# A hybrid attention block on one core: helper work moved in the prologue and the first slots, pairs turned in one transfer, and another order of the last products

## The chip, the cores and the metric

The kernel runs on one core of a Trainium2 chip. Five engines work side by side and wait for one another by semaphores: TensorE (PE; its weight loads are listed apart as PEld), VectorE (DVE), ScalarE (ACT), GpSimd (POOL) and SyncE (SP), which here issues the DMAs, plain ones and transposes. Each engine takes its instructions in the order in which they were written for it. The metric is the time of one execution on the device, in microseconds (us).

## The reference

x is 2048 rows of 1024 float32. It is normalised (RMS norm with a gain) and projected at once to the queries, keys and values of two attention mixers, to gates, and to merge gates:

```python
PROJ_SIZES = (A_WIDTH, A_KV_HEADS * HEAD_DIM, A_KV_HEADS * HEAD_DIM,
              len(B_GROUPS) * B_WIDTH, len(B_GROUPS) * B_WIDTH, len(B_GROUPS) * B_WIDTH,
              A_WIDTH, B_WIDTH, N_BRANCHES * D_MODEL)
```

Mixer A is a banded attention of 8 query heads over 2 key heads (window 128 to each side) with a sink logit; mixer B has three groups of 8 heads with dilations 1, 4 and 16, whose results are combined by their softmax denominators. Queries and keys get an RMS norm per head; a relative-position bias is added to the logits. Each mixer's output is gated, projected to 1024 columns, weighted by the merge gates, added up, and a last projection of it is added to x.

## The kernel before

Every matrix product is done in fp16 in three parts: each operand is split into a high and a low half (names ending in h and l, or XH and XL for the normalised x), and high x high, high x low and low x high are added up in PSUM. The program has these stages.

*Prologue* (0 to about 80 us). x is loaded in 16 tiles, normalised (xt, L462), turned by TensorE (L482), and split into XH by ScalarE (L485) and XL by VectorE (L489). Two pieces of the gate projection (L352) run between. The functions `x_again` (GpSimd copies the first columns of XH and XL behind the last ones, since a shifted unit reads past the end), `head_gain` (the rows by which the heads' norms are weighted, some ten small VectorE operations a call) and `small_scales` are helpers. A small planner, the class `Order`, is given each step with its engine, an assumed duration, what it depends on and a rank, and writes the steps out in the order that results.

*Attention* in units of 8 slots. An A unit holds four query heads and one key head, a B unit two heads of one dilation; the first three units are A, B, A. In each slot TensorE projects one pair of 128-row subsets (L697). The queries and keys of it are normalised (rw, spl, with GpSimd's steps L764 and L779) and turned by DMA transposes into the tiles kq by `Pair.turn` (L787). Then come the items of earlier pairs: logits s<-kq (L847), row maxima (L862), exponentials, high and low half p (L879), the DMA transpose of p to pt (L885), the values pv<-vt,pt (L896), and later the output: z and zd, yo, ya, and a turn on TensorE pt<-idf,ya (L960) into the bank also used for small column sums (pt<-ym,ones at L189), which VectorE reads in the gate L967.

Helpers that belong to no slot are put into a heap by `at(t, ...)` with a time counted in slots, and each is written out when the written-out work has come so far. The tables at the head of the file (W_STEP, Y_MAX, L_LAST and others) hold these times. So the order in which an engine, or SyncE's queue, gets its work follows from those numbers. The transposes of pair k are written at slot k + 2.24. The loads of the raw weights of the next unit (wraw, L178, four pieces of 384 KB, written two by two) stand at 0.1 and 0.6 slots into a unit. Squares of them, for the scale of their high half, follow at 1.9.

*Middle and last stage.* Seven-product matrix multiplication (Strassen's) with the two branch projections and the output projection. Classes `Branch` (L1921) and `Out` (L1993) hold seven products each; `run(g)` writes them as 0, 1, 2, 3, 4 and leaves 5 and 6 in a list `pending`, from which `late()` takes one between products of the next group, and `flush()` the rest. Products 0, 1 and 2 start a fresh bank of PSUM, 3, 5 and 6 add to the bank of product 0, and 4 to that of 2. After each product VectorE or ScalarE reads the bank (`after`): in `Out` it is added to a tile xr of x (L2000), which is then stored (L2003).

Of the kernel before, what the change touches and what calls it, by code (L numbers as in the profile page):

```python
# [21 lines left out]
F32 = mybir.dt.float32  # L22
F16 = mybir.dt.float16
# [11 lines left out]
HD = 64  # L35
# [10 lines left out]
def unit_order():  # L46
    us = [("A", 0, 0)]
    for p in range(4):
        us.append(("B", p, 1))
        if p == 0:  # L50
# [20 lines left out]
W_STEP = (0.1, 0.6, 1.9, 0.445, 4.186, 0.117, 0.301)  # L71
W_MAX = (3.542, 3.596)
G_PREP = (5.907,)
N_PREP = (5.948, 6.756, 7.277)
Y_MAX = (0.02, 0.445, 0.485)
# [7 lines left out]
W_RAW, L_LAST = 14.0, 0.3  # L83
# [16 lines left out]
            gh=1.06, gl=1.26, mm=.217, th=.6, gt=.63, us=.83, uh=.75, ul=.82, ag=1.0, tl=1.3)  # L100
XT_BUFS = 14
KQ_BUFS = 6
# [6 lines left out]
def block_kernel(tc, x, w_units, w_gate, w_mrg, w_out, w_bra, w_brk, gain, qkg, sink, bias_a, bias_b, b_merge, out):  # L109
# [301 lines left out]
    qg = sp0.tile([128, 4, HD], F32, name="qg")  # L411
# [148 lines left out]
    for t in range(NT):  # L560
# [15 lines left out]
        if t < 2:  # L576
            for k in range(2):
                od.add(("ag", t, k), "G", us_["ag"], [("lo", t, 1)], 0, x_again, t, (XH, XL)[k])
# [37 lines left out]
    od.add("h0", "V", 1.6, [("st", groups[7])], 170, head_gain, 0, first=46.0)  # L616
    od.add("h1", "V", 1.6, ["h0"], 170, head_gain, 1)
    od.add("ss", "V", .2, ["h1"], 171, small_scales)
# [61 lines left out]
    class Pair:  # L680
# [100 lines left out]
        def turn(self):  # L781
            for i, s in enumerate(self.subsets):
                if self.un.shift and s[1] == 0:
                    kq = wk.tile([128, 6, 128], F16, name="kq0", bufs=3)
                else:
                    kq = wk.tile([128, 6, 128], F16, name="kq", bufs=KQ_BUFS)
                nc.sync.dma_start_transpose(out=kq[:], in_=self.sp[:, i].rearrange("p a b c -> p (a b c)"))  # L787
                self.un.kq[s] = kq
# [415 lines left out]

    ws, fill = {}, {}
    w_forms(NU + SEQ[0][0], 8 * NU)
    for u in range(NU + 1):
        t = 8 * u
        steps = [(t + W_STEP[i], w_load, u + 1, (2 * i, 2 * i + 1)) for i in range(2)]
        for i in range(4):  # L1210
            steps.append((t + W_STEP[2] + W_STEP[3] * i, w_square, u + 1, i))
# [662 lines left out]
    def run(g):  # L1874
        emit(g, 0)
        if g.n == 1:
            late()
            return
        emit(g, 1)
        late()  # L1880
        emit(g, 2)
        emit(g, 3)
        late()
        emit(g, 4)
        pending.extend(((g, 5), (g, 6)))
# [89 lines left out]
    class Out(Seven):  # L1975
# [11 lines left out]
        def matmuls(self, i, ps, fresh):  # L1987
            m = mf[self.s, i]
            out = []
            for p in range(4):  # L1990
# [14 lines left out]

        def after(self, i):
            b = self.b
            for h, n, k, store in (((0, 0, 0, False),), ((1, 1, 2, False),), ((0, 0, 1, True),), ((0, 1, 0, False),),
# [7 lines left out]
    def AB(s):  # L2016
# [7 lines left out]
        run(Branch(s, 1))  # L2024
# [98 lines left out]
```

## Time and profile before

| | us |
|---|---|
| Median of 3 runs | 1914.71 (1913.5 to 1917.62) |
| The profiled execution | 1916.55 |
| its span, first to last instruction | 1914.3 |
| TensorE busy in it | 1873.9 |
| VectorE, ScalarE, GpSimd busy | 1500.7, 1250.4, 579.0 |

The mean granted clock of TensorE was 0.999. A row of a timeline holds the start, the duration, the engine, the line, the operation, the tiles (out<-in), the shape, the count, and in brackets the idle time ahead of it with what ended it. Rows of SPq are what SyncE itself needs to issue a DMA; when the data lands is listed apart. A line of the list of waits has the idle time in all, how often, and the longest.

### The profile page before, as it was taken

To read this page: it belongs to the slowest core of one execution; us is meant where nothing else is said; L and a number is where in the kernel's file an instruction comes from. 1 tells how busy PE (TensorE), PEld (TensorE's weight loads), DVE (VectorE), ACT (ScalarE), POOL (GpSimd) and SP (SyncE) were. 2 spreads that over 40 slices of the span, in tenths; PEclk is the share of its full clock that TensorE was granted. 3 is DMA by queue.
4 is the path that set the end of the run, shared out by engine and by line. 5 is a ranking of instruction groups with operands and counts; after the bars stand their busy time and mean duration, and the time that the engine had idled before them with its cause. 6 is when DMAs were issued, how large, how long until landed. Compare 5 with 4: busy or idle time off the path is not lost.

```text
span 1914.3 us, 51103 instructions
## 1 busy us (share of the span) xinstructions
PE 1873.9 (98%) x19242; PEld 1438.9 (75%) x19242; DVE 1500.7 (78%) x3835; ACT 1250.4 (65%) x3015; POOL 579.0 (30%) x1363
## 2 busy tenths in 40 slices
PE   6999999999999999999999999999999999999998
PEld 4567887889999899998999899544444446776774
DVE  7679878986887879878788888748679644987885
ACT  8577768887676777777776766565666865433431
POOL 1034343443454435534455444300000001322121
PEclk9999999999999999999999999999999999999999
DMA  6259998988889679888897777786666648854541
GB/s 256 83 98 197 164 185 134 192 161 178 149 161 181 134 158 200 151 170 169 143 179 144 147 154 132 165 309 172 211 198 188 190 156 273 290 164 122 148 148 65
DMA packets 639351, 326.21 MB, mean 170 GB/s; under 512 B 459264, under 2 KB 589952, under 8 KB 636672
## 3 DMA queue, kind: packets, MB, share of 16 engines
q1 hardware_dynamic: 638960, 322.70, 73.3%
q8 instruction: 150, 2.46, 0.6%
q14 instruction: 97, 0.79, 0.2%
q10 hardware_dynamic: 144, 0.26, 0.0%
HBM read 139.08 MB, written 73.66 MB: 111 GB/s over the span
## 4 chain that ended last, share of the span: by engine, by line
PE 90%; DMA 5%; DVE 2%; ACT 1%; issue 1%; POOL 0%; SPq 0%; DVEq 0%; POOLq 0%
PE pj L697 43%; PE fps L1602 17%; PE fps L1921 8%; PE fps L1993 8%; PE s L847 5%; PE pv L896 4%; DMA pt<-p 2%; PE pj L352 2%; PE pj L304 1%; PE fps L304 1%; DMA kq<-spl 1%; PE pt L960 1%; DMA bigl<-sd 1%; DVE pr L862 0%; PE s L482 0%
## 5 line engine op out<-in xcount | busy, mean ns | idle before, releaser
L697 PE MATMUL pj<-wl,XH 128*128 128x128 f16 (+2 forms) x2816 | 715.8, 268 | 0.0
L697 PE MATMUL pj<-wh,XL 128*128 128x128 f16 (+2 forms) x2816 | 712.2, 269 | 0.0
L697 PE MATMUL pj<-wh,XH 128*128 128x128 f16 (+2 forms) x2816 | 709.4, 268 | 0.0
L697 PEld LDWEIGHTS <-XH 128*128 128x128 f16 x5632 | 575.3, 112 | 54.5
L697 PEld LDWEIGHTS <-XL 128*128 128x128 f16 x2816 | 315.9, 112 | 24.0
L862 DVE CUSTOM_DVE_ANT_0 pr<-s,b,ubuf 128x256 f32<-128x256 f32 (+3 forms) x512 | 218.9, 465 | 44.1 <-PE s L847 41.7
L879 DVE SCALAR_TENSOR_TENSOR p<-pr,p 128x512 f16<-128x512 f32 (+2 forms) x256 | 195.7, 765 | 51.6 <-ACT p L875 50.4
L764 POOL TENSOR_TENSOR rw<-rw,g 128x128 f32<-128x128 f32 (+1 forms) x224 | 149.1, 686 | 202.5 <-DVE rw L757 183.2
L1931 POOL TENSOR_TENSOR g<-g,t 128x512 f32<-128x512 f32 x32 | 48.8, 1526 | 523.7 <-DVE t L1854 523.7
L1602 PEld LDWEIGHTS <-wh 128*128 128x128 f16 x1064 | 104.1, 99 | 123.5 <-issue 0.4
L715 ACT ACTIVATE rw<-pj 128x256 f32<-128x256 f32 (+1 forms) x224 | 87.5, 390 | 134.5 <-PE pj L697 134.0
L779 POOL COPY spl<-spl 128x256 f16<-128x256 f16 (+1 forms) x224 | 96.4, 460 | 246.5 <-DVE spl L774 246.5
L875 ACT ACTIVATE p<-pr 128x512 f16<-128x512 f32 (+2 forms) x256 | 157.7, 616 | 14.4 <-DMA pt<-p 10.1
L1921 PE MATMUL fps<-y,bigh 128*128 128x128 f16 x1792 | 153.5, 219 | 0.8 <-DVE r L1854 0.8
L847 PE MATMUL s<-kq 128*128 128x128 f16 (+1 forms) x1856 | 148.2, 218 | 4.8 <-DMA kq<-spl 3.9
L1921 PE MATMUL fps<-y,bigl 128*128 128x128 f16 x896 | 151.7, 219 | 0.0
L1993 PE MATMUL fps<-WO,mf 128*128 128x512 f16 x672 | 150.3, 379 | 0.8 <-DVE xr L2000 0.8
L847 PEld LDWEIGHTS <-kq 128*128 128x128 f16 x2016 | 131.0, 98 | 21.1 <-issue 5.7
L1921 PEld LDWEIGHTS <-bigh 128*128 128x128 f16 x1792 | 139.0, 98 | 8.2 <-issue 0.9
L896 PE MATMUL pv<-vt,pt 128*128 128x65 f16 (+1 forms) x2784 | 132.1, 193 | 8.7 <-DMA pt<-p 7.7
L896 PEld LDWEIGHTS <-pt 128*128 128x128 f16 x3024 | 119.6, 98 | 24.6 <-DMA pt<-p 12.5
L770 ACT ACTIVATE spl<-rw 128x512 f16<-128x512 f32 (+1 forms) x112 | 72.1, 643 | 79.7 <-POOL vt L726 71.4
(252 smaller groups left out, 3815.0 us busy)
## 6 DMA issues: line engine op xcount, KB each, us to landing
wraw<-in_w_units_dram SPq DMA_DIRECT2D x56, 384.0 KB, 4.8
g<-mgd SPq DMA_DIRECT2D x64, 256.0 KB, 5.4
wraw<-in_w_mrg_dram SPq DMA_DIRECT2D x45, 256.0 KB, 4.2
mgd<-t SPq DMA_DIRECT2D x43, 256.0 KB, 2.9
zd<-z SPq DMA_DIRECT2D x128, 66.0 KB, 2.0
zz<-zd SPq DMA_DIRECT2D x64, 132.0 KB, 3.5
xt<-in_x_dram SPq DMA_DIRECT2D x16, 512.0 KB, 7.8
ytd<-yo SPq DMA_DIRECT2D x32, 256.0 KB, 3.5
```

Source lines behind the costliest of these rows:

```text
L697: out.append(lambda lhs=lhs, rhs=rhs, ch=ch, a=a, b=b, k=k: T.matmul(ps[:, a:b], lhsT=lhs[:, ch, :], rhs=rhs[:, ch, a:b], start=(k == 0), ...
L715: A.activation(self.rw[:, n * i:n * i + n], self.ps[i][:, :n], AF.Copy)
L764: G.tensor_tensor(q[:, i, :un.nq, :], q[:, i, :un.nq, :], g, OP.mult)
L779: G.tensor_copy(sp[:, i, nh:, :, :], sp[:, i, nq:nh, ::-1, :])
L847: T.matmul(self.sv[j][:, o:o + k1 - k0], lhsT=q[:, h, :], rhs=kt[:, un.nq + kh + v * un.nk, k0:k1], start=(v == 0), stop=(v == 1))
L862: V.tensor_tensor_reduce(out=self.pv[:, j, self.p0:self.p0 + W], in0=self.sv[j], in1=un.bias[:, self.h0 + j, self.b0:self.b0 + W], scale=I ...
L875: A.activation(self.sp[:, :128 * n], self.pr, AF.Copy, scale=PSC)
L879: V.scalar_tensor_tensor(self.sp[:, 128 * n:], self.pr, PSC, self.sp[:, :128 * n], OP.mult, OP.subtract)
L896: T.matmul(self.po[:, j, :w], lhsT=p[:, n * j + s, :], rhs=un.v[key][:, vh, c0:c0 + w], start=(k == 0 and s == 0), stop=(k == 2 and s == n ...
L1602: T.matmul(b[k][:], lhsT=w[:, i, ch, :], rhs=xform(PROD[i][0], lo, ch, q), start=(i < 3 and n == 0), stop=(n == 11), skip_group_check=True)
L1921: out.append(lambda p=p, c=c, wl=wl, yl=yl, n=n: T.matmul(ps[:, 128 * p:128 * p + 128], lhsT=w[wl][:, i, c, p, :], rhs=y[:, yl, c, :], sta ...
L1993: out.append(lambda p=p, ml=ml, wl=wl, k=k: T.matmul(ps[:], lhsT=m[:, ml, p, :], rhs=WO[:, i, wl, p, :], start=(fresh and k == 0), stop=(k ...
```

## The change

It has seven parts. The copies `x_again` leave the planner and are written in slots 0.9, 1.4, 1.9 and 2.4 of the attention; `head_gain` and `small_scales` leave it too, for slots 0.1, 0.35 and 0.45 (the tile qg moves to a pool that lives as long). The weight loads of unit 2 are written 1.9 slots earlier, its squares half a slot. Two entries of Y_MAX, which place the column sums over ym, get smaller by 0.065. L_LAST, a delay of the last pair's logits in slots, goes from 0.3 to 0.4. The tile kq holds a whole pair, four of them instead of six for one subset, and in an A unit one transpose of 12 blocks fills it instead of two of 6; B units keep two. In the last Branch and Out the products run 0, 1, 3, 2, 5, 4, 6, and the last product of all is computed in two halves of 256 columns, the first into a fresh bank, each half added and stored by itself.

```diff
@@ -69,10 +69,11 @@
 Y_PART = (-0.02, 0.571, 0.797, 0.981, 1.031)
 GATE = (-0.062, 0.084, 0.255)
 W_STEP = (0.1, 0.6, 1.9, 0.445, 4.186, 0.117, 0.301)
+W_SOON = (1.9, .5)
 W_MAX = (3.542, 3.596)
 G_PREP = (5.907,)
 N_PREP = (5.948, 6.756, 7.277)
-Y_MAX = (0.02, 0.445, 0.485)
+Y_MAX = (0.02, 0.38, 0.42)
...
...
-W_RAW, L_LAST = 14.0, 0.3
+W_RAW, L_LAST = 14.0, 0.4
...
+X_AG, H_AT = .9, (.1, .35)
 XT_BUFS = 14
-KQ_BUFS = 6
+KQ_BUFS = 4
 VT_BUFS = 10
 PT_BUFS = 4
 N_BIAS_A = 384
...
     sp0 = st.enter_context(tc.tile_pool(name="sp0", bufs=1))
-    qg = sp0.tile([128, 4, HD], F32, name="qg")
+    qg = cst.tile([128, 4, HD], F32, name="qg")
     snk = cst.tile([128, 8], F32, name="snk")
     nsnk = cst.tile([128, 8], F32, name="nsnk")
     bmt = cst.tile([128, 16], F32, name="bmt")
@@ -573,9 +575,6 @@
                    10 * t + X_XR[1], x_turn, t, h)
             od.add(("hi", t, h), "A", us_["hi"], [("tr", t, h)], 10 * t + X_XR[2], x_hi, t, h)
             od.add(("lo", t, h), "V", us_["lo"], [("hi", t, h)], 10 * t + X_XR[3], x_lo, t, h)
-        if t < 2:
-            for k in range(2):
-                od.add(("ag", t, k), "G", us_["ag"], [("lo", t, 1)], 0, x_again, t, (XH, XL)[k])
     for c in range(2):
         r = X_GR[c]
         od.add(("gq", c), "A", us_["sq"], [("ld", f"w{c}", 0)], r, g_square, c, first=X_GF[c])
@@ -613,9 +612,6 @@
         od.add(("ul", i), "V", us_["ul"], [("uh", i)], 160 + i, w_lo, 0, i)
     od.add("um", "T", .15, [("uq", i) for i in range(4)] + [("gp", 1)], 150, w_sum, 0)
     od.add("up", "V", us_["pw"], ["um", "gs"], 150, w_pow, 0)
-    od.add("h0", "V", 1.6, [("st", groups[7])], 170, head_gain, 0, first=46.0)
-    od.add("h1", "V", 1.6, ["h0"], 170, head_gain, 1)
-    od.add("ss", "V", .2, ["h1"], 171, small_scales)
     od.run()
     until(1e9)
     st.close()
@@ -779,13 +775,16 @@
                 G.tensor_copy(sp[:, i, nh:, :, :], sp[:, i, nq:nh, ::-1, :])
 
         def turn(self):
+            kq = wk.tile([128, 12, 128], F16, name="kq", bufs=KQ_BUFS)
+            outs = [kq[:, 6 * i:6 * i + 6] for i in range(2)]
+            if self.un.shift and self.un.n == NT and self.subsets[0][1] == 0:
+                outs[0] = wk.tile([128, 6, 128], F16, name="kq0", bufs=1)[:]
+            if self.un.kind == "A":
+                nc.sync.dma_start_transpose(out=kq[:], in_=self.sp[:].rearrange("p s a b c -> p (s a b c)"))
             for i, s in enumerate(self.subsets):
-                if self.un.shift and s[1] == 0:
-                    kq = wk.tile([128, 6, 128], F16, name="kq0", bufs=3)
-                else:
-                    kq = wk.tile([128, 6, 128], F16, name="kq", bufs=KQ_BUFS)
-                nc.sync.dma_start_transpose(out=kq[:], in_=self.sp[:, i].rearrange("p a b c -> p (a b c)"))
-                self.un.kq[s] = kq
+                if self.un.kind == "B":
+                    nc.sync.dma_start_transpose(out=outs[i], in_=self.sp[:, i].rearrange("p a b c -> p (a b c)"))
+                self.un.kq[s] = outs[i]
 
 
     class Item:
@@ -1202,13 +1201,19 @@
             at(t + F_AT[2] + F_AT[3] * i + F_AT[4], lo, i)
         at(t + F_AT[5], w_load, NU + SEQ[2][0])
 
+    for b, k in enumerate(H_AT):
+        at(k, head_gain, b)
+    at(H_AT[1] + .1, small_scales)
+    for k in range(4):
+        at(X_AG + .5 * k, x_again, k // 2, (XH, XL)[k % 2])
     ws, fill = {}, {}
     w_forms(NU + SEQ[0][0], 8 * NU)
     for u in range(NU + 1):
         t = 8 * u
-        steps = [(t + W_STEP[i], w_load, u + 1, (2 * i, 2 * i + 1)) for i in range(2)]
+        ahead = W_SOON if u == 1 else (0.0, 0.0)
+        steps = [(t + W_STEP[i] - ahead[0], w_load, u + 1, (2 * i, 2 * i + 1)) for i in range(2)]
         for i in range(4):
-            steps.append((t + W_STEP[2] + W_STEP[3] * i, w_square, u + 1, i))
+            steps.append((t + W_STEP[2] + W_STEP[3] * i - ahead[1], w_square, u + 1, i))
             if u < NU:
                 steps += [(t + W_STEP[4] + W_STEP[3] * i, w_hi, u + 1, i),
                           (t + W_STEP[4] + W_STEP[5] + W_STEP[3] * i, w_lo, u + 1, i)]
@@ -1871,18 +1876,19 @@
         if pending:
             emit(*pending.pop(0))
 
-    def run(g):
+    def run(g, final=False):
         emit(g, 0)
         if g.n == 1:
             late()
             return
         emit(g, 1)
         late()
-        emit(g, 2)
-        emit(g, 3)
+        for i in (3, 2) if final else (2, 3):
+            emit(g, i)
         late()
-        emit(g, 4)
-        pending.extend(((g, 5), (g, 6)))
+        for i in (5, 4) if final else (4,):
+            emit(g, i)
+        pending.extend(((g, 6),) if final else ((g, 5), (g, 6)))
 
     def flush():
         while pending:
@@ -1987,6 +1993,19 @@
         def matmuls(self, i, ps, fresh):
             m = mf[self.s, i]
             out = []
+            if (self.s, i) == (7, 6):
+                fb = bank()
+                for h in range(2):
+                    c, o = slice(256 - 256 * h, 512 - 256 * h), (fb[:, :256], ps[:, :256])[h]
+                    for p in range(4):
+                        for ml, wl in ((0, 0), (0, 1), (1, 0)):
+                            k = len(out)
+                            out.append(lambda p=p, ml=ml, wl=wl, c=c, o=o, h=h, k=k: T.matmul(
+                                o, lhsT=m[:, ml, p, :], rhs=WO[:, i, wl, p, c], start=(k == 0), stop=(k % 12 == 11),
+                                skip_group_check=True))
+                    if h == 0:
+                        out.append(lambda: self.half(1, fb[:, :256]))
+                return out
             for p in range(4):
                 for ml, wl in ((0, 0), (0, 1), (1, 0)):
                     k = len(out)
@@ -2003,8 +2022,20 @@
                 at(now[0] + 1.0, lambda: nc.sync.dma_start(
                     out=out[t0:t0 + 128, 512 * n:512 * n + 512], in_=t[:]))
 
+        def half(self, j, b, store=True):
+            c, t0 = slice(256 * j, 256 * j + 256), 128 * self.s + 1024
+            t = self.x[1, 0]
+            V.scalar_tensor_tensor(t[:, c], b, i_o[:], t[:, c], OP.mult, OP.add)
+            if store:
+                nc.sync.dma_start(out=out[t0:t0 + 128, c], in_=t[:, c])
+
         def after(self, i):
             b = self.b
+            if (self.s, i) == (7, 6):
+                self.half(0, b[0][:, :256])
+                return
+            if (self.s, i) == (7, 5):
+                at(now[0] + .4, lambda: self.half(1, b[0][:, 256:], False))
             for h, n, k, store in (((0, 0, 0, False),), ((1, 1, 2, False),), ((0, 0, 1, True),), ((0, 1, 0, False),),
                                    ((0, 1, 2, True),), ((1, 1, 0, True),), ((1, 0, 0, True),))[i]:
                 self.put(h, n, b[k], store)
@@ -2021,7 +2052,7 @@
             for i in range(7):
                 at(p + WO_AT[0] + WO_AT[1] * i, wo_load, i)
         run(Branch(s, 0))
-        run(Branch(s, 1))
+        run(Branch(s, 1), s == 7)
 
     AB(0)
     at(pos[0] + 9, outs[0].load, ((0, 0), (1, 1), (0, 1), (1, 0)))
@@ -2038,7 +2069,7 @@
             at(p + (31.1 if s < 6 else 28.0), outs[s + 1].load, ((1, 0),))
         if s == 6:
             flush()
-        run(outs[s])
+        run(outs[s], s == 7)
         if s < 6:
             AB(s + 2)
     flush()
```

SyncE's queue in slots 6 and 7 of the first A unit, before. kq<-spl are the transposes of a pair, pt<-p those of an item, yo a load, b a bias.

```order
L885 DMA_TRANSPOSE pt_1762<-p_1722 128x12x128
L787 DMA_TRANSPOSE kq<-spl 128x6x128 x2
L885 DMA_TRANSPOSE pt_1844<-p_1795 128x12x128
L885 DMA_TRANSPOSE pt_1909<-p_1868 128x12x128
L885 DMA_TRANSPOSE pt_1975<-p_1935 128x12x128
...
L885 DMA_TRANSPOSE pt_2317<-p_2266 128x12x128
L178 DMA wraw<-in_w_units_dram 128x768 x2
L787 DMA_TRANSPOSE kq<-spl 128x6x128 x2
L946 DMA yo<-gtd_88 128x512
L885 DMA_TRANSPOSE pt_2417<-p_2357 128x12x128
```

The same piece of the queue in the changed kernel, where the line numbers are a few off:

```order
L884 DMA_TRANSPOSE pt_1754<-p_1714 128x12x128
L180 DMA wraw<-in_w_units_dram 128x768 x2
L783 DMA_TRANSPOSE kq<-spl 128x12x128
L884 DMA_TRANSPOSE pt_1837<-p_1787 128x12x128
L884 DMA_TRANSPOSE pt_1902<-p_1861 128x12x128
L180 DMA wraw<-in_w_units_dram 128x768 x2
L884 DMA_TRANSPOSE pt_1970<-p_1928 128x12x128
...
L884 DMA_TRANSPOSE pt_2310<-p_2259 128x12x128
L783 DMA_TRANSPOSE kq<-spl 128x12x128
L945 DMA yo<-gtd_88 128x512
L884 DMA_TRANSPOSE pt_2405<-p_2347 128x12x128
```

The loads moved from ahead of the pair at 172.94 us to ahead of the pair at 145.68 us, and their second half from behind the transpose at 178.79 to behind that at 150.36; each pair is one row of 12 blocks.

TensorE at the logits of the last pair, before (pj are projections, of which one in three parts is one row each; weight loads and equal rows are left out):

```order
L304 MATMUL pj<-XL,wh 128x512
...
L847 MATMUL s<-kq 128x128
...
L304 MATMUL pj<-XH,wl 128x512
...
L896 MATMUL pv<-vt,pt_24044 128x65
...
L304 MATMUL pj<-XH,wh 128x512
...
L960 MATMUL pt<-idf,ya 128x128 x4
```

And in the changed kernel:

```order
L306 MATMUL pj<-XH,wl 128x512
...
L895 MATMUL pv<-vt,pt_23921 128x65
...
L306 MATMUL pj<-XH,wh 128x512
...
L959 MATMUL pt<-idf,ya 128x128 x4
...
L846 MATMUL s<-kq 128x128
```

The eight rows s<-kq moved behind one projection, the twelve pv, two projections and the turn of ya.

GpSimd's first rows behind the set-up, before:

```order
L493 COPY XH<-XH 128x8x128
L493 COPY XL<-XL 128x8x128
L493 COPY XH<-XH 128x8x128
L493 COPY XL<-XL 128x8x128
L726 MEMSET vt 128x1 x2
L264 TENSOR_TENSOR rs_t<-rs_y 128x10
...
L764 TENSOR_TENSOR rw<-rw,g 128x256 x2
```

And in the changed kernel:

```order
L722 MEMSET vt 128x1
L495 COPY XH<-XH 128x8x128
L722 MEMSET vt 128x1
L266 TENSOR_TENSOR rs_t<-rs_y 128x10
...
L495 COPY XL<-XL 128x8x128
L722 MEMSET vt 128x1
L760 TENSOR_TENSOR rw<-rw,g 128x256 x2
L495 COPY XH<-XH 128x8x128
L722 MEMSET vt 128x1
L775 COPY spl<-spl 128x128 x2
```

Three of the four copies now stand among GpSimd's steps for the first pair, the fourth among those of the second.

## The prediction

> **What bounds the kernel now.** First the busy times of the page and the list of TensorE's waits (in that view: us in total, times, longest).
>
> ```profile
> PE 1873.9 (98%) x19242; PEld 1438.9 (75%) x19242; DVE 1500.7 (78%) x3835; ACT 1250.4 (65%) x3015; POOL 579.0 (30%) x1363
> ...
> PE s L482 <- DVE xss L445: 10.7, 1, 10.7
> PE s L847 <- DMA kq<-spl: 3.9, 3, 1.6
> PE pj L352 <- ACT XH L485: 2.1, 2, 1.7
> ```
>
> TensorE is busy for 1873.9 of 1914.3 us. The change adds and removes no arithmetic on it, so all that can be won is a part of its 40 us of idle time, and of the few microseconds behind its last matmul. The wait of 10.7 us for the first tiles of x stays. What is left is a list of single waits, which I take in order of time.
>
> The second view is the timeline of the first 20 us, with the statistics of two VectorE lines (ns: least, median, most).
>
> ```profile
> 17.25 1.04 POOL L493 COPY XH<-XH 128x1024 f16<-128x1024 f16 x1
> ...
> 17.32 2.04 DVE L462 SCALAR_TENSOR_TENSOR xt<-xt,xr,gb 128x1024 f32<-128x1024 f32 x1
> ...
> 19.51 1.94 PE L482 MATMUL s<-idf,xt 128*128 128x128 f32 x8 [4.00 <-DVE wm L196]
> ...
> L462 DVE SCALAR_TENSOR_TENSOR xt<-xt,xr,gb x16: 1276/1280/2040, 9.3 to 67.5; 128x1024 f32<-128x1024 f32 x16
> L458 DVE TENSOR_SCALAR xr<-xr,ubuf x6: 215/230/984, 9.0 to 56.8; 128x4 f32<-128x4 f32 x3, 128x1 f32<-128x1 f32 x2, 128x2 f32<-128x2 f32 x1
> ```
>
> The transposes at 19.51 need the tile xt, which L462 finishes at 19.36; the name in the bracket is of the instruction beside it. That L462 took 2.04 us, 0.76 over its median, beside the third of GpSimd's four copies and the fourth, and the longest L458 took 0.98, 0.75 over its median. So 1.5 us of the 4.00 come from VectorE being held up beside GpSimd's copies.
>
> **The change, part by part.**
>
> *Copies and head rows moved.* Taking GpSimd's four copies out of the prologue lets TensorE start its second stretch up to 1.5 us earlier. Whether that lasts depends on ScalarE, for which TensorE waits later in the prologue (2.1 us in the list above); if ScalarE cannot move along, the gain is 0. I take **1.0**, two thirds, bounds 0 and 1.5. The copies then run in the first slots:
>
> ```profile
> 95.68 1.41 POOL L764 TENSOR_TENSOR rw<-rw,g 128x256 f32<-128x256 f32 x2 [1.21 <-DVE rw L757]
> ...
> 99.09 2.65 SPq L787 DMA_TRANSPOSE kq<-spl  x2
> ...
> 104.91 0.61 PE L847 MATMUL s<-kq 128*128 128x128 f16 x8
> ```
>
> A copy of 1.04 us fits the 1.21 us in which GpSimd waits for VectorE ahead of rw. If each of two copies holds VectorE up by 0.76 on the way to the first pair's transposes, these go out 1.5 us late. They land some 3 us after 99.09 (the row of landings stands below) and are first used at 104.91, which leaves a cover of about 3 us. So I cost the copies at nothing, and likewise the 22 small VectorE operations of the head rows, which now run in the first half slot, ahead of this same pair; with the cover gone the copies would cost up to 1.5 once.
>
> [...]
>
> *Unit 2's loads moved, and one 12-block transpose for two of 6.* The third view is SyncE's queue in slots 4 to 8 of the attention, and what TensorE and VectorE do at its ends.
>
> ```profile
> 145.68 2.94 SPq L787 DMA_TRANSPOSE kq<-spl  x2
> 148.78 9.45 SPq L885 DMA_TRANSPOSE pt<-p  x4
> ...
> 171.44 1.41 SPq L178 DMA_DIRECT2D wraw<-in_w_units_dram  x2
> 172.94 2.67 SPq L787 DMA_TRANSPOSE kq<-spl  x2
> ...
> 176.34 1.43 SPq L885 DMA_TRANSPOSE pt<-p  x1
> ...
> 181.83 1.04 SPq L178 DMA_DIRECT2D wraw<-in_w_units_dram  x2
> ...
> 188.90 3.41 SPq L787 DMA_TRANSPOSE kq<-spl  x2
> ```
>
> ```profile
> 171.40 0.96 DVE L879 SCALAR_TENSOR_TENSOR p<-pr,p 128x768 f16<-128x768 f32 x1 [0.19 <-ACT p L875]
> ...
> 154.21 0.38 PE L896 MATMUL pv<-vt,pt 128*128 128x65 f16 x7 [0.67 <-DMA pt<-p]
> 182.42 0.35 PE L896 MATMUL pv<-vt,pt 128*128 128x65 f16 x6 [1.91 <-DMA pt<-p]
> 201.89 0.34 PE L896 MATMUL pv<-vt,pt 128*128 128x65 f16 x3 [2.03 <-DMA pt<-p]
> ```
>
> The list of waits again, first between 140 and 210 us and then between 320 and 390 (the second A unit), and the statistics of the two kinds of transposes (L787 from 99 to 200 us, L885, 12 blocks each, from 136 to 160), each with its line of landing times.
>
> ```profile
> PE pv L896 <- DMA pt<-p: 5.5, 5, 2.0
> ...
> PE pv L896 <- DMA pt<-p: 2.2, 4, 0.7
> ...
> L787 SPq DMA_TRANSPOSE kq<-spl x16: 1212/1260/2356, 99.1 to 190.2; - x16
> DMA to landing us min/median/max: 2.7/3.0/4.6
> ...
> L885 SPq DMA_TRANSPOSE pt<-p x8: 1412/1441/2441, 136.8 to 156.8; - x8
> DMA to landing us min/median/max: 3.7/3.9/5.4
> ```
>
> The p for the transpose at 176.34 was written by 172.36, so it stood 4 us behind others in SyncE's queue. Without the loads (1.41 and 0.09 between) and with one transpose of 1.44 in place of 2.67, it goes out 2.7 us earlier, at 173.6; with 3.9 to landing that is 177.5, and TensorE wanted it at 180.5. The 1.91 goes, with 3 us to spare. The other late waits of this stretch (5.5 - 0.67 - 1.91 = 2.9 us) stand behind the second load (1.04) and behind the pair of 188.90, which takes 3.41 now and by the row of 12 blocks 1.44; I let 0.7 of the whole 4.8 stay and take a gain of 4.1.
>
> Against this stands the new place. The first two loads now go ahead of the transposes of 145.68. For SyncE that is even: 1.04 to 1.41 and 1.44 instead of 2.94, so the p transposed at 148.78 is issued when it was. But 768 KB are ahead of it in the queue. The nearest row is the longest landing of L787, 4.6 us against a median of 3.0: that is the pair directly behind the loads at 172.94. So it lands 1.6 later, and since TensorE waited 0.67 for it already, nothing covers that: a loss of 1.5, with bounds of 0 (the loads fit between) and 2.8. The second two go out ahead of the p of 153.90, which has more room. Net for this stretch **2.6**, bounds 0 (the loads' delay returns at each of the next transposes) and 5.5.
>
> In the second A unit only the merging acts: each pair frees about 2 x 1.26 - 1.44 = 1.1 us of SyncE ahead of the p behind it. Of 2.2 us in four waits I take **1.3**; bounds 0 and 2.2. B units keep their two transposes: nothing.
>
> *Y_MAX.* Fourth, the turn at 255 us.
>
> ```profile
> 258.77 0.35 PE L189 MATMUL pt<-ym,ones 128*128 128x1 f32 x2 [0.94 <-DVE yo L967]
> ...
> 256.10 0.42 DVE L862 CUSTOM_DVE_ANT_0 pr<-s,b,ubuf 128x192 f32<-128x192 f32 x1 [1.16 <-PE s L847]
> ```
>
> The sum over ym waits because the turn ahead of it holds the PSUM bank until VectorE's gate L967 has read it. Now the sum stands ahead of the turn, and the six small operations on it fall into VectorE's 1.16 us of idle time. The turn must wait for one short read; estimate 0.2. Gain **0.75**, bounds 0 and 0.94.
>
> *L_LAST.* Fifth, the last pair.
>
> ```profile
> 1204.86 3.82 SPq L787 DMA_TRANSPOSE kq<-spl  x2
> ...
> 1208.76 0.42 DVE L1066 TENSOR_TENSOR ya<-ya,zz 128x256 f32<-128x256 f32 x1
> ...
> 1210.15 0.49 PE L847 MATMUL s<-kq 128*128 128x128 f16 x6 [1.60 <-DMA kq<-spl]
> 1211.49 0.60 PE L960 MATMUL pt<-idf,ya 128*128 128x128 f32 x4
> ```
>
> TensorE waits 1.60 us for the second half of the last pair. In the new order one projection, the twelve pv, two projections and the turn come first: all that ran from 1210.49 to 1211.93, 1.44 us. The turn would start at about 1209.3, and its ya is ready at 1209.18. Gain **1.3**, bounds 0.4 (ya late by 0.9) and 1.45.
>
> *The end.* Sixth, the last stage's two waits, its last VectorE operation, and a VectorE row of half the width.
>
> ```profile
> 1871.85 0.27 PE L1921 MATMUL fps<-y,bigh 128*128 128x128 f16 x2 [0.78 <-DVE r L1854]
> 1907.87 2.75 PE L1993 MATMUL fps<-WO,mf 128*128 128x512 f16 x12 [0.84 <-DVE xr L2000]
> ...
> 1910.65 0.75 DVE L2000 SCALAR_TENSOR_TENSOR xr<-fps,ubuf,xr 128x512 f32<-128x512 f32 x1 [2.84 <-PE fps L1993]
> ...
> 1844.78 0.48 DVE L1763 SCALAR_TENSOR_TENSOR y<-tq,ubuf,y 128x256 f16<-128x256 f32 x1
> ...
> out_dram<-xr SPq DMA_DIRECT2D x6, 256.0 KB, 2.0
> ```
>
> Product 6 waits in both places until VectorE has read product 5 out of the bank that both use. With 5 ahead of 4 that read has 2.6 us. Gain 0.78 + 0.84. The last VectorE operation is half as wide: 0.75 - 0.48 = 0.27. For the store of 128 KB instead of 256 no row gives a time; between nothing and half of 2.0 I take nothing. The 24 matmuls of 256 columns cost what twelve of 512 did, if their weight loads stay hidden. Together **1.9**, bounds 1.2 and 2.9.
>
> *Sum.* 1.0 + 2.6 + 1.3 + 0.75 + 1.3 + 1.9 = 8.85. The profiled execution took 1916.55 (span 1914.3, 2.25 around it), so it would take 1907.7. It lies 1.84 above the median of the runs, 1914.71; from there the forecast is **1905.9**. The lower ends add up to 1.6 and the upper ones to 14.5.
>
> **The rivals.** (a) *The loads only move the waits.* The transfers of slots 4 to 8 are the same bytes in the same stretch, so TensorE waits at 150 to 165 for what it now waits for at 180 to 202; the first two terms and the A unit's give nothing, and 0.75 + 1.3 + 1.9 = 4.0 is left: 1910.7. For it: the first p after the loads has no slack (0.67 wait). Against it: at 176.34 the queue of SyncE was late, not only the transfers. [...]
>
> (b) *Slower: the first half of each pair arrives too late.* A 12-block transpose lands 3.9 us after issue against 3.0 for one of 6, so the half that is used first comes 0.9 later, in 16 pairs of the two A units. If TensorE stood at all of them, that is 14.4 us, against 8.85 gained: 1914.71 + 5.6 = 1920.3. It decides from the point where the time from landing to first use is under 0.9, plus what the loads add. Against it: the first pair lands 3 us ahead of use, and the three waits for kq in the list (3.9 us in all) include none of the A units' pairs. For it: with the copies' 1.5 and 0.9 late, the first pair has only 0.6 left.
>
> (c) *The gain of the prologue and the tail only.* VectorE's own load in the slots (it is at 78% over the span) holds the p's back, the early p's help nothing: 1.0 + 0.75 + 1.3 + 1.9 = 4.95, 1909.8.
>
> **How the numbers follow.** A difference of 0.2% (3.8 us) is about what a measurement can tell from none: faster is below 1910.9. I give the forecast 0.55, (a) 0.2, (b) 0.1 and (c) 0.15. The forecast is faster nearly always (0.53 of 0.55, with its small terms at the low ends it falls within 0.2%), (a) is at the border and half of it (0.1) counts as the same, (c) lies 1.1 below the border, and of it 0.1 counts as faster. Of (b) three quarters end slower; the rest, with few pairs late, is the same. Faster 0.73, same 0.19, slower 0.08. The range: from the forecast down to where half of the remaining bounds (14.5 - 8.85 = 5.65) come true, 1903, and a little below, 1902; up over (c) and (a), with 3 us more for one part of (b), 1914.
>
> **What the profile after would show.** Right: no copy L493 before 80 us and the transposes of 19.51 near 18.0; wraw ahead of the kq of 145 and no wait over 1 us between 170 and 205; a wait of 1.5 to 2.5 us near 153; a sum over ym without a wait at 258; the s<-kq wait of 1208 under 0.4 us; no wait of product 6 in the last 45 us. Wrong: waits for kq in slots 1 to 8, or for pt at 150 to 165 of over 3 us in all; then (b) or (a) holds. The forecast fails above all if the transfers, not SyncE's queue, set the landings.

## The result, and the profile after

| | before | after |
|---|---|---|
| Median, us | 1915.3 (1913.5 to 1918.9, 6 runs) | 1905.65 (1902.31 to 1906.95, 6 runs) |
| The profiled execution, us | 1916.55 | 1904.35 |
| its span, us | 1914.3 | 1902.3 |
| Ratio of the runs | | 0.9945, 95% interval 0.9932 to 0.9958 |

A second measurement, in the last set of experiments, gave 1906.96 and 0.9959 (0.9946 to 0.9972). The forecast was 1905.9. First the list of TensorE's waits in the kernel after (us in all, times, longest):

```profile
PE s L846 <- DMA kq<-spl: 4.7, 5, 1.4
PE pv L895 <- DMA pt<-p: 4.1, 5, 1.3
PE s L484 <- DVE wm L198: 2.5, 1, 2.5
PE pj L354 <- ACT XH L487: 2.4, 2, 1.9
PE pt L191 <- ACT wl L215: 1.1, 1, 1.1
PE fps L191 <- ACT tq L1457: 1.0, 1, 1.0
```

The waits for pt fell from 7.7 to 4.1 us, those for kq rose from 3.9 to 4.7, and the lines for the gate, for r and for xr are gone. The prologue's wait of 4.00 us is 2.48. VectorE is no longer held up there: of the sixteen operations that make xt, the longest took 2.04 us before and takes 1.285 now, with the median at 1.28 in both (least, median and most, in ns):

```profile
L464 DVE SCALAR_TENSOR_TENSOR xt<-xt,xr,gb x16: 1274/1280/1285, 9.2 to 64.3; 128x1024 f32<-128x1024 f32 x16
```

What follows the wait differs too. Here is TensorE's timeline of the kernel after, and then the same matmuls in the kernel before:

```profile
17.86 1.94 PE L484 MATMUL s<-idf,xt 128*128 128x128 f32 x8 [2.48 <-DVE wm L198]
...
22.67 1.89 PE L354 MATMUL pj<-XH,gh 128*128 128x512 f16 x8 [0.49 <-ACT XH L487]
```

```profile
24.33 3.57 PE L352 MATMUL pj<-XH,gh 128*128 128x512 f16 x8 [0.41 <-ACT XH L485]
...
24.00:28.00 4.00, 3.67 (x10) 1.32 (x10) 3.61 (x15) 3.94 (x9) 0.00 (x0) 1.00 1.02 412
200.00:205.00 5.00, 3.11 (x30) 2.58 (x31) 2.71 (x9) 2.92 (x6) 0.85 (x5) 0.69 1.16 172
```

The first eight gate matmuls take 3.57 us before and 1.89 after. The two lower rows are the windows view of the kernel before (length, busy time of PE, PEld, DVE, ACT, POOL with the number of operations, granted clock, DMA share, GB/s). In 200 to 205 us, behind the wait of 2.03, the granted clock is 0.69; in 24 to 28 us the column says 1.00, though the matmuls there run at half the rate. So the difference between these two executions, 12.0 us of span, holds about 1.7 us at 24 us, and a slow stretch of 3.4 us behind 201.9, worth some 1.6, neither of which a term of the sum had counted.

SyncE's queue after, with the loads moved, and TensorE at that place:

```profile
142.41 1.37 SPq L180 DMA_DIRECT2D wraw<-in_w_units_dram  x2
143.83 2.62 SPq L783 DMA_TRANSPOSE kq<-spl  x1
146.63 5.42 SPq L884 DMA_TRANSPOSE pt<-p  x2
152.10 1.05 SPq L180 DMA_DIRECT2D wraw<-in_w_units_dram  x2
```

```profile
150.56 0.44 PE L846 MATMUL s<-kq 128*128 128x128 f16 x5 [1.42 <-DMA kq<-spl]
...
152.77 0.41 PE L895 MATMUL pv<-vt,pt 128*128 128x65 f16 x8 [1.12 <-DMA pt<-p]
...
180.72 0.44 PE L895 MATMUL pv<-vt,pt 128*128 128x65 f16 x9 [1.35 <-DMA pt<-p]
...
1201.61 0.61 PE L846 MATMUL s<-kq 128*128 128x128 f16 x8
```

The pair's transpose behind the loads, issued at 143.83, lands 6.7 us later, at about 150.5: TensorE waits 1.42 us for it and then 1.12 for the p behind, where 0.67 had been. The wait of 1.91 at 182 us is still 1.35, and those of 0.56, 0.37 and 2.03 shrink to one of 0.48. The last pair's logits at 1201.61 wait for nothing. At the end the last VectorE operation and the stores are shorter, and 24 matmuls of 256 columns take what twelve of 512 took (2.75):

```profile
1896.30 2.78 PE L2003 MATMUL fps<-WO,mf 128*128 128x256 f16 x24
...
1899.12 0.48 DVE L2028 SCALAR_TENSOR_TENSOR xr<-fps,ubuf,xr 128x256 f32<-128x256 f32 x1 [0.82 <-PE fps L2003]
...
out_dram<-xr SPq DMA_DIRECT2D x2, 128.0 KB, 1.8
```

### The profile page after: what moved, and what is told of

Read it like the earlier page. It is cut to its first block, busy times and chain, and to the rows that moved or that the text cites. A ratio compares the mean times of both kernels' runs of the same rounds, so it can differ in the third digit from the quotient of the medians.

```text
span 1902.3 us, 51104 instructions
## 1 busy us (share of the span) xinstructions
PE 1869.9 (98%) x19254; PEld 1439.0 (76%) x19254; DVE 1499.3 (79%) x3837; ACT 1249.5 (66%) x3015; POOL 579.6 (30%) x1363
## 4 chain that ended last, share of the span: by engine, by line
PE 89%; DMA 5%; ACT 2%; DVE 2%; issue 1%; POOL 0%; SPq 0%; DVEq 0%; POOLq 0%; ACTq 0%
PE pj L693 42%; PE fps L1607 18%; PE fps L1927 8%; PE fps L2012 7%; PE s L846 5%; PE pv L895 4%; DMA pt<-p 2%; DMA kq<-spl 2%; PE pj L306 2%; PE pj L354 1%; PE fps L306 1%; ACT jk L443 1%; PE pt L959 1%; DMA bigl<-sd 1%; PE s L484 0%
```

## The experiments

| Kernel | median, us | ratio to before, 95% interval | in us |
|---|---|---|---|
| before with copies and head rows moved | 1912.58 | 0.9989 (0.9980 to 0.9998) | -2.1 |
| before, TensorE kept busy in its first wait | 1915.9 | 1.0001 (0.9991 to 1.0012) | 0.2 |
| after, loads at the old place | 1902.98 | 0.9936 (0.9920 to 0.9953) | -12.2 |
| after, two transposes of 6 blocks | 1908.63 | 0.9971 (0.9957 to 0.9986) | -5.6 |
| after, old end | 1907.49 | 0.9965 (0.9953 to 0.9977) | -6.7 |
| after, old Y_MAX and L_LAST | 1908.55 | 0.9973 (0.9962 to 0.9984) | -5.2 |
| after, old prologue | 1907.0 | 0.9964 (0.9951 to 0.9976) | -6.9 |
| after, loads late | 1907.53 | 0.9969 (0.9960 to 0.9978) | -5.9 |
| after, again | 1906.96 | 0.9959 (0.9946 to 0.9972) | -7.8 |
| after, loads at the old place, again | 1903.52 | 0.9946 (0.9934 to 0.9958) | -10.3 |
| after, loads one by one | 1905.2 | 0.9950 (0.9935 to 0.9966) | -9.6 |
| before with merged transposes alone | 1909.83 | 0.9978 (0.9969 to 0.9987) | -4.2 |

The last column is the ratio's distance from 1 times 1914. The sets were measured at different times (the kernel before had medians of 1914.55, 1913.63 and 1913.95 in them), so ratios are compared, not medians, except within a set.

**The prologue alone.** Two parts of the change put into the kernel before:

```diff
-        if t < 2:
-            for k in range(2):
-                od.add(("ag", t, k), "G", us_["ag"], [("lo", t, 1)], 0, x_again, t, (XH, XL)[k])
...
+    for b, k in enumerate((.1, .35)):
+        at(k, head_gain, b)
+    at(.45, small_scales)
+    for k in range(4):
+        at(.9 + .5 * k, x_again, k // 2, (XH, XL)[k % 2])
```

> The kernel before with one part of the change alone: the GpSimd copies and the head rows go to the first slots. Theory (two effects: 1.5 us of VectorE hold-up, and the TensorE clock, which stays at full rate because the wait is 2.5 instead of 4.0 us): the first gate matmuls of 128x512 take 0.215 us each instead of 0.43, TensorE is 3.2 to 3.4 us earlier at the wait for nmA near 130 us, and the whole is 3 us shorter than before, or some more or less by how the waits of the first A unit fall. Rival (hold-up alone, as the prediction had it): 1.5 us earlier at 130 us, 1.0 to 1.5 in all.

Measured: 0.9989, -2.1 us (0.4 to 3.8), which lies between the 3 us of the theory and the 1.0 to 1.5 of the rival and tells neither from the other. Its profile has the theory's signs, the wait of 2.48 and fast gate matmuls. It also shows that a long wait need not be followed by a slow stretch: behind 3.05 us the projections take 0.22, where the kernel before has 0.30 behind its wait of 2.03 (second fence).

```profile
17.89 1.94 PE L482 MATMUL s<-idf,xt 128*128 128x128 f32 x8 [2.48 <-DVE wm L196]
...
198.07 0.71 PE L890 MATMUL pv<-vt,pt 128*128 128x65 f16 x18 [3.05 <-DMA pt<-p]
198.63 0.22 PE L691 MATMUL pj<-wh,XH 128*128 128x128 f16 x1
```

```profile
202.86 0.30 PE L697 MATMUL pj<-wh,XH 128*128 128x128 f16 x1
```

**TensorE kept busy.** Transposes of no use ahead of the third tile:

```diff
         xps[t, h] = ps = s_p.tile([128, 4, 128], F32, name="s")
+        for c in range(12 if (t, h) == (2, 0) else 0):
+            T.transpose(ps[:, c % 4, :], idf[:], idf[:])
```

> The kernel before with twelve transposes of the identity added, of no use to the result, in TensorE's wait of 4.0 us ahead of the third tile of x; they last 2.9 us and end before that tile is ready. Theory (clock): the wait itself stays (the third tile starts near 19.5), but the first gate matmuls take 0.215 instead of 0.43 us, and TensorE is 1.6 to 2 us earlier from 30 us on; 1.7 in all. Rival (the slow matmuls come of the transfers and of ScalarE at that time, not of the idle time ahead of them): they stay at 0.43 and the time is that of before.

```profile
15.99 2.82 PE L481 MATMUL s<-idf 128*128 128x128 f32 x12 [0.75 <-DVE XL L491]
19.15 1.09 PE L484 MATMUL s<-idf,xt 128*128 128x128 f32 x8 [0.34 <-DVE xt L462]
...
23.54 1.89 PE L352 MATMUL pj<-XH,gh 128*128 128x512 f16 x8 [0.67 <-ACT XH L487]
```

The profile is what the theory wanted: the eight turns of the third tile take 1.09 instead of 1.94 us, the gate matmuls 1.89, and TensorE is 2.4 us earlier at 28 us. The time is not: 1.0001. The interval reaches to a gain of 1.7 us (0.9991) and no further. So this run does not show the clock to be worth anything to the whole. Nor does it show it to be worth nothing: the three profiled kernels that start with the wait of 4.0 us have 8, 5 and 0 slow gate matmuls (below), 0.9 us in the mean, and a gain of that size lies within the interval. The next runs show why the comparison of two profiles had misled me.

**The old prologue in the kernel after.**

```diff
+    for t in range(2):
+        for k in range(2):
+            od.add(("ag", t, k), "G", us_["ag"], [("lo", t, 1)], 0, x_again, t, (XH, XL)[k])
...
-    for k in range(4):
-        at(X_AG + .5 * k, x_again, k // 2, (XH, XL)[k % 2])
```

> The changed kernel with the copies and the head rows back in the prologue. The same part alone was worth 0.11% (2 us) on the kernel before, while TensorE was 3.3 us earlier at 130 us. Theory (the waits of the first A unit ate the rest, and merged transposes let it through): 3.0 to 3.4 us longer than the changed kernel. Rival (always swallowed to that extent): 2 us longer; by the prediction's term: 1.0.

Measured 0.9964; the changed kernel had 0.9945 and 0.9959, which puts the part at 3.6 or 1.0 us. The intervals overlap, so that the time alone does not even tell it from nothing, and the theories aren't told apart. The profile settles the other point. The wait is 4.00 us again, and yet the gate matmuls are fast:

```profile
19.19 1.94 PE L484 MATMUL s<-idf,xt 128*128 128x128 f32 x8 [4.00 <-DVE wm L198]
...
24.01 1.89 PE L354 MATMUL pj<-XH,gh 128*128 128x512 f16 x8 [0.52 <-ACT XH L487]
```

while two kernels with the short wait have them slow, the one with the loads at the old place (second run)

```profile
17.74 1.94 PE L484 MATMUL s<-idf,xt 128*128 128x128 f32 x8 [2.48 <-DVE wm L198]
...
22.56 3.52 PE L354 MATMUL pj<-XH,gh 128*128 128x512 f16 x8 [0.42 <-ACT XH L487]
25.91 1.89 PE L354 MATMUL pj<-XL,gh 128*128 128x512 f16 x8
```

and the one with the loads one by one:

```profile
17.80 1.94 PE L485 MATMUL s<-idf,xt 128*128 128x128 f32 x8 [2.48 <-DVE wm L199]
...
23.02 3.57 PE L355 MATMUL pj<-XH,gh 128*128 128x512 f16 x8 [0.82 <-ACT XH L488]
26.38 2.68 PE L355 MATMUL pj<-XL,gh 128*128 128x512 f16 x8
```

Counting the gate matmuls at half rate in every profile gives 8 and 5 in two kernels with the wait of 4.0 and 0 in the third; and with the wait of 2.48 it gives 0, 0, 0, 0, 0, 2, 3, 4, 8 and 12. My theory of the clock, that the shorter wait keeps it, has fallen: the moment at which TensorE gets fast lies anywhere between 22 and 28 us, at the same work.

With as many slow matmuls on both sides, what the part itself gives can be read. The first logits of the attention start at 103.0 us in this kernel and at 101.7 in the changed one (no slow matmul in either), and at 104.9 in the kernel before and 103.0 in the one with the loads at the old place, second run (eight in each): 1.3 and 1.9 us, about the 1.5 by which VectorE was held up. And the hold-up is back here: the longest operation that makes xt takes 2.04 us again, where it takes at most 1.29 in the ten kernels that have the part.

**The loads at the old place.**

```diff
-W_SOON = (1.9, .5)
+W_SOON = (0.0, 0.0)
```

> The changed kernel with unit 2's weight loads and squares at their old times. Theory: the wait for kq near 149 us (1.42) and that for pt behind it (1.12) go, the late waits at 180 to 202 come back in part (the merged transposes alone take 1.1 to 2 us off them), with a stretch at half clock if one is 2 us or longer: 1 to 3 us longer than the changed kernel. Rival (the merged transposes were enough): no late wait over 1 us, 2 us shorter than the changed kernel.

> The changed kernel without the earlier weight loads, a second time, beside the changed kernel on the same chip. Theory after the first run (the earlier place wins nothing, since it moves the waits from 177 to 202 us to 149 to 153): 0 to 2 us shorter than the changed kernel. Rival (the prediction's term): 1 us or more longer.

Measured 0.9936 and 0.9946, where the changed kernel has 0.9945 and 0.9959; in the set that holds both, 1903.52 against 1906.96. The intervals of the ratios overlap. Within that set the means of six executions each differ by 2.6 us (an estimate of its 95% interval from their spread: 0.6 to 4.5). So the earlier loads win nothing, and may cost some 2 us. The waits between 140 and 225 us, for the changed kernel again and then for the second run without the earlier loads:

```profile
PE pv L895 <- DMA pt<-p: 3.6, 4, 1.2
PE s L846 <- DMA kq<-spl: 1.7, 1, 1.7
```

```profile
PE pv L895 <- DMA pt<-p: 4.9, 5, 2.0
```

5.3 and 4.9 us: the earlier loads turn late waits into early ones and win nothing. The prediction's term for the moved loads falls. The rival of the first run, that the merged transposes were enough, has the time right but not the profile: it expected no late wait over 1 us, and the longest is 1.8 in the first run and 2.0 in the second. The p that the late wait at 180 us is for shows why. Here is its row in the chain of work that ended last, in the kernel before and then in the second run (issue, us to landing):

```profile
176.34 6.04 DMA pt<-p
```

```profile
173.21 6.60 DMA pt<-p
```

Counted from the moment at which TensorE wants it, this transpose goes out 4.2 us ahead in the kernel before, 4.7 to 4.9 ahead in the three kernels with merged transposes and the loads at the old place, and 4.3 ahead in the changed one; it lands 6.0, 6.5 to 6.6 and 5.6 us after issue. TensorE waits 1.91, 1.66 to 1.92 and 1.35 us for it.

**Two transposes of 6 blocks, and the merging alone.** In the changed kernel, the old `Pair.turn` with six tiles; in the kernel before, the new one with four:

```diff
-            kq = wk.tile([128, 12, 128], F16, name="kq", bufs=KQ_BUFS)
...
-            if self.un.kind == "A":
-                nc.sync.dma_start_transpose(out=kq[:], in_=self.sp[:].rearrange("p s a b c -> p (s a b c)"))
             for i, s in enumerate(self.subsets):
...
+                    kq = wk.tile([128, 6, 128], F16, name="kq", bufs=KQ_BUFS)
+                nc.sync.dma_start_transpose(out=kq[:], in_=self.sp[:, i].rearrange("p a b c -> p (a b c)"))
```

> The changed kernel with two transposes of 6 blocks for each pair of an A unit, and the old tiles for kq. Theory (SyncE's queue is the limit): the four waits of the second A unit (2.2 us before, 0.6 after) come back, those of the first grow by 1 to 2 us: 2.5 to 4 us longer than the changed kernel; the new waits for kq near 745 and 969 us stay. Rival (the bytes are the limit, two transposes or one are the same): no difference above 1 us; and if the four pair tiles made the waits near 745 and 969, these are gone here.

> The kernel before with one part alone: one transpose of 12 blocks for a pair of an A unit, and the pair tiles. Theory (SyncE's queue was late from 160 to 202 us): 3 to 5 us shorter than before, by the run with this part undone (which was 0.26% longer than the changed kernel), with less wait at 180 to 202 and in the second A unit. Rival (the prediction's terms, which put most of the first A unit's gain down to the loads): 1.3 in the second unit and about 1 in the first, 2 to 2.5 us in all.

Undone, 0.9971 against 0.9945 and 0.9959, 3.6 us by the mean of the two; alone, 0.9978, that is 4.2 us (2.5 to 5.9). Both are what the theories said. The part is one transfer and the larger tiles together; these were not taken apart. The waits between 130 and 225 us with the part undone:

```profile
PE pv L892 <- DMA pt<-p: 6.1, 6, 1.7
```

and with the merging alone, in the windows that the prediction showed, 140 to 210 us and 320 to 390:

```profile
PE pv L899 <- DMA pt<-p: 3.7, 3, 1.7
...
PE pv L899 <- DMA pt<-p: 0.8, 2, 0.5
```

5.5 and 2.2 us had become 3.7 and 0.8, with the loads where they were. One pair of profiles says too much here. In the second A unit the waits with the part undone did not come back, as expected, to 2.2 but are 0.7, and 0.7 more for ScalarE; in the four profiles without merging they are 2.2, 1.8, 1.3 and 0.7, in the ten with it 0.3 to 1.0. From 140 to 225 us those for the two transposes are 5.1 to 6.2 without merging and 2.8 to 5.3 with it. By the means, then, merging takes about 1.4 us of waits in the first A unit and 0.8 in the second; where the rest of the 4.2 us comes from is not shown. With the six tiles TensorE still waits for kq in B units (1.5 us at 728 and 0.9 at 973), so the four pair tiles don't make such waits, which the changed kernel has at 745 and 969 us.

**The loads late, and one by one.**

In the first the loads stand at slots 10.2 and 10.3, and the squares of them come later too:

```diff
-W_SOON = (1.9, .5)
+W_SOON = (-2.2, -1.05)
...
-        steps = [(t + W_STEP[i] - ahead[0], w_load, u + 1, (2 * i, 2 * i + 1)) for i in range(2)]
+        steps = [(t + W_STEP[i] * (.2 if u == 1 else 1) - ahead[0], w_load, u + 1, (2 * i, 2 * i + 1)) for i in range(2)]
```

> The changed kernel with unit 2's weight loads neither sooner nor at the old place but at slots 10.2 and 10.3, around the pair issued near 200 us, of which the first use lies 12 us behind its landing; the squares 1.05 slots later. Theory (any place in slots 5 to 9 of the A unit puts 1.5 MB in front of transposes that have no slack): neither the waits at 149 to 153 nor the one over 1 us at 177 remain; 1.5 to 3 us shorter than the run without the earlier loads (1903 there), 4 us shorter than the changed kernel. Rival (the bytes of the transposes alone make the late waits): the time of the run without the earlier loads.

In the second they are written one by one:

```diff
+W_FOUR = (5.8, 6.05, 6.6, 6.85)
...
+        if u == 1:
+            steps = [(k, w_load, u + 1, (i,)) for i, k in enumerate(W_FOUR)]
```

> The changed kernel with unit 2's four loads one by one, at slots 5.8, 6.05, 6.6 and 6.85, none directly ahead of a pair's transposes or of the first p behind them. Theory (a load costs only where what follows it has less slack than its 0.8 to 1.5 us): the wait for kq near 149 and that for pt behind it go, no wait of over 1 us from 145 to 165; 1 to 2.5 us shorter than the changed kernel. Rival (the transfers of this stretch are at their limit, and any place only moves the wait): within 1 us of the changed kernel.

The late ones gave 0.9969, longer than the changed kernel, against both the theory (4 us shorter) and the rival (the time with the loads at the old place). The waits moved to 194 and 206 us, and TensorE waited for the sum of the later squares too (140 to 225 us):

```profile
PE pv L895 <- DMA pt<-p: 5.0, 3, 3.0
PE pt L191 <- ACT wl L215: 1.5, 1, 1.5
```

One by one they gave 0.9950, 1905.2 beside 1906.96 and 1903.52. Its wait for pt is down to 1.4 us from 140 to 215 us, as the theory had it (a wait of 1.4 follows between 215 and 225):

```profile
PE pv L896 <- DMA pt<-p: 1.4, 2, 0.9
PE pv L896 <- ACT rs_y L258: 0.8, 1, 0.8
```

but the whole isn't shorter than with the loads at the old place, within what these runs can tell; four executions do not tell the theory (1 to 2.5 us) from the rival (within 1).

**The old end, and the old Y_MAX and L_LAST.** One run each, in the changed kernel:

```diff
-Y_MAX = (0.02, 0.38, 0.42)
+Y_MAX = (0.02, 0.445, 0.485)
...
-W_RAW, L_LAST = 14.0, 0.4
+W_RAW, L_LAST = 14.0, 0.3
```

```diff
-        run(Branch(s, 1), s == 7)
+        run(Branch(s, 1))
...
-        run(outs[s], s == 7)
+        run(outs[s])
```

(and in the second the halves of the last product as one). In each run two things are undone together, so that the time gives their sum alone.

> The changed kernel with Y_MAX and L_LAST as before. Theory: the wait of 0.94 us for the gate at about 250 us and the wait of 1.4 to 1.6 us at the last pair come back; 2.1 us longer than the changed kernel (0.75 and 1.3 by the prediction). Rival (the time won there is waited out later): no difference above 0.5 us.

> The changed kernel with the last Branch and Out in the old order and the last product in one piece. Theory (the end lies behind everything, so its gain is what the profile says): the waits of 0.78 and 0.84 us come back, the last VectorE operation is 0.75 long, 2.3 us longer than the changed kernel (the prediction had 1.9). Rival (part of it is hidden): less than 1 us.

0.9973 and 0.9965. Against the mean of the two measurements of the changed kernel (0.9952) these are 4.0 and 2.5 us, against the later one 2.7 and 1.1. Worked out from the intervals of the three ratios, the 4.0 carry an uncertainty of 2.7 us, so that the rival of that run (the time is waited out later) falls; the 2.5 carry one of 2.9, and that time decides nothing. The waits are back in the timelines, with the tables old

```profile
252.00 0.35 PE L191 MATMUL pt<-ym,ones 128*128 128x1 f32 x2 [0.94 <-DVE yo L966]
1203.41 0.49 PE L846 MATMUL s<-kq 128*128 128x128 f16 x6 [2.38 <-DMA kq<-spl]
```

and with the end old:

```profile
1859.38 0.27 PE L1927 MATMUL fps<-y,bigh 128*128 128x128 f16 x2 [0.78 <-DVE r L1859]
1895.39 0.81 PE L2012 MATMUL fps<-WO,mf 128*128 128x512 f16 x3 [0.84 <-DVE xr L2019]
```

**The changed kernel again.**

> The changed kernel itself, unaltered, on one chip with the three others of this set. Earlier sets had it at 0.9945 of the kernel before, and the four kernels with one part undone at 0.9964 to 0.9973; the parts so measured add up to more than the whole. Theory (the parts add up, with tail 2.3, Y_MAX and L_LAST 2.1, prologue 2 to 3, merging 3 to 4, loads 0 to -2): 0.9945 to 0.9955. Rival (the first measurement was a lucky one): 0.996 or more.

0.9959 lies between the theory (up to 0.9955) and the rival (0.996 or more): the first measurement was at the good end. With the mean, 0.9952 or 9.2 us, the parts undone (2.3 for the prologue, 3.6 for the merging, 4.0 for the tables, 2.5 for the end) and -2 for the loads make 10.4. That agrees, but the intervals are wide: each of these parts is uncertain by about 3 us.

## Why the prediction was right

The time came out at the forecast (1905.65 and 1906.96; said 1905.9), and the two waits at the tables, the two at the end and the prologue's hold-up went as the rows had said. That it came out to within a microsecond is luck: the six executions of one measurement lie 4 to 5 us apart, and one step of the sum is wrong and was covered by others.

- *Prologue, 1.0.* The wait shrank from 4.00 to 2.48 in every kernel with this part, by the 1.5 us of hold-up that the rows gave; ScalarE moved along (TensorE's waits for it are 2.4 us, 2.1 before). Alone it was worth 2.1 us (0.4 to 3.8), which allows both the 1.0 and the full 1.5. The copies in the slots cost no wait, as said: the first pair now lands 1.7 us ahead of its use, at 100.0 us, where it was 3.0. One of the four copies still ran early, at 61.9 us.
- *Loads and merging, 2.6 in the first A unit.* The net is about right, its parts are not. The step that failed is "it goes out 2.7 us earlier, at 173.6; with 3.9 to landing that is 177.5", and with it the gain of 4.1 for which I counted the new place of the loads as needed. The 3.9 was the median of transposes from 136 to 160 us; the one in question landed 6.0 us after issue before the change already, and 5.6 to 6.6 after. Nor did it go out 2.7 us earlier against the moment at which TensorE wants it, but 0.15 with the loads moved, since the pair's transpose ahead of it took 4.21 us to issue and not 1.44, and 0.5 to 0.7 with the loads at the old place. So 1.35 of the 1.91 stayed. That the transfers, and not SyncE's queue alone, set the landings there is what the prediction had named as its weakest point; why they are slow there was not tested. Rival (a) was right about the loads and wrong about the merging.
- *What the two are worth.* Merging alone brought 4.2 us of time; the loads' new place brought nothing, and perhaps took 2 us back. Its price was seen, but at the wrong transfer: I expected the p behind the pair to be late by 1.6, and the pair itself was late first, landing 6.7 us after issue, where the three pairs ahead of it took 3.6 to 3.8. Why it took that long behind the loads is not shown.
- *Second A unit, 1.3.* 2.2 us of waits became 0.6 in the two profiles, but by the profiles of all kernels only about 0.8 of that is the merging's.
- *Y_MAX 0.75 and L_LAST 1.3.* The wait for the gate is 0.9 us in all five profiles with the old table and gone in the nine others. That of the last pair is 1.4 to 2.4 with the old L_LAST and 0 to 0.6 with the new one. The time says 2.7 to 4.0 for the two.
- *The end, 1.9.* 0.78 and 0.84 are there in every profile with the old end and in none with the new, with 0.27 at the last operation, and 0.2 in the store that I had left out (1.8 against 2.0).
- *Rivals (b) and (c).* The only A pair that TensorE waits for is the one behind the loads; the three kernels with merged transposes and the loads at the old place show no such wait, so 0.9 us more of landing is covered. VectorE did not hold the p's back to the point where earlier ones help nothing, since the merging alone won time.

Two of the signs that the prediction named did not come: a wait of 1.35 us is left between 170 and 205, and near 153 it is 1.12 and not 1.5 to 2.5. And a sign of being wrong came, a wait for kq within the first A unit, 1.42 us. It is rival (a)'s cost of the loads and not (b)'s.

The kernel without the earlier loads had the lowest medians of this case: 1902.98 and 1903.52.

## What to carry to other kernels

Where one queue issues many small transposes and stands full, as here, try one transfer of twice the blocks: it cost little more to issue (a median of 1.50 us against 1.26, up to 200 us) and was worth 4.2 us, while each of the new places for the loads mostly moved the wait. A time to landing is to be read from the transfer in question, and not from a quieter stretch: 3.9 was 6.0 here. A pair of products that share a bank should have another product between them (without one TensorE waited 0.78 and 0.84 us here, with one it did not), above all at the end, where nothing comes later to take the gain back. And the difference of two profiles is one draw of each: read from it which waits are there, look for them in the profiles of all kernels, and take the size of a gain from many runs.

## What was not expected of the hardware

TensorE starts slow in these executions: in the kernel after, eight turns of x take 1.94 us at 10.6 us and 1.04 at 28.5. Its first gate matmuls of 128x512 take about 0.43 us for a while and 0.215 then, and the change came between 22 and 28 us in 13 executions with nearly the same work ahead of it; 0 to 12 matmuls were slow, worth up to 2.6 us (12 times 0.215). Behind a wait of 2.03 us near 200 us it was slow for 3.4 us in one execution, behind 3.05 in another not at all. What sets the moment of the change was not shown. It spreads over 6 us, with TensorE working in bursts before 22 us, and the length of the wait ahead does not order it: 8, 5 and 0 slow matmuls behind 4.0 us, 0 to 12 behind 2.48. The spread may be a good part of the 3 to 5 us by which executions of one kernel differ; that was not tested by itself. The column of the granted clock showed it at 200 us (0.69) and not at 24 us (1.00).
